# Operand chunks copied from PSUM by ScalarE, and six pairs by seven products in place of four

## The chip, the cores and the metric

The kernel runs on one core of a Trainium2 chip. The metric is device time in microseconds of one execution, as the median of a few runs. A core has five engines with instruction queues of their own: TensorE (PE in the profile; its weight loads are shown apart as PEld), VectorE (DVE), ScalarE (ACT), GpSimd (POOL) and SyncE (SP), which here issues nearly all transfers from memory. Data is computed on in SBUF; TensorE writes its results to PSUM, which has eight banks of 128 x 512 f32. This kernel keeps four banks for the sums of a product (`ps_acc`) and four for everything else (`ps_tmp`).

## The reference

One layer of an encoder block, on 256 rows (`T`) of 4096 columns (`D`), all in f32. What matters here is the chain of large products:

```
xn   = rms_norm(x)
proj = xn @ w_in                       # 4096 -> 14336: q, k, v, z_a, a_c, g_c, z_c
y_a  = rms_norm(attention(q, k, v)) * silu(z_a)          # 2048 columns
y_c  = rms_norm(conv_module(a_c, g_c)) * silu(z_c)       # 2048 columns
h    = x + concat(y_a, y_c) @ w_out                      # 4096 x 4096
gate = sigmoid(rms_norm(h) @ w_ple_gate + b_ple_gate)    # 4096 x 4096
out  = rms_norm(h + gate * (p @ w_ple))
```

The change touches the making of the left operands of two of them: `concat(y_a, y_c)` for w_out (the projection) and `h` for w_ple_gate (the last gate), and the order of work in the first product of each.

## The kernel before

**A product.** `mixed_product` computes two column blocks of 512 for both halves of the rows (four quarters, h = row half, j = column block) over the 4096 rows of a weight, which it takes in 16 pairs of 128-row blocks. Every f32 operand is split into a high part in the rounded format f32r and a low part (the rest, again f32r), and a product of two blocks is three matmuls: high x high, low x high, high x low (`add`, L380 to L391, the matmul at L385). The high part of a weight is made by ScalarE and the low part by VectorE (`parts_of`, L204 and L205); three tiles of each exist (`part_tiles`).

**Plain pairs and sevens.** A plain pair does 2 blocks x 4 quarters x 3 matmuls = 24 (`add_plain`). A pair marked `*` is done as a 2 x 2 block product with seven multiplications in place of eight (Strassen's scheme in Winograd's form): 7 x 3 = 21 matmuls. For this VectorE makes sums of the weights (`ua`, `ub`, L467, L468, L474, L475) and splits them, and the left operand's combinations of the pair's four blocks must stand ready in a second operand tile (`comb`, read by `s_of`). Three of the seven products (P2, P3, P4) go to the product's own banks, as three of a plain pair's four quarters do; the other four (P1, P5, P6, P7, the helpers) take all four `ps_tmp` banks from the first seven of a product until `on_helpers` has summed them after its last seven (`helper_sums`, L512 to L516, and sums of the caller).

**The orders.** A string such as `dense` gives the order of the 16 pairs and marks the sevens. `late` (L340) is used for the first of the four products of w_out and for the first of the four of the last gate: there the left operand is still being made while the product runs, and it is made in `ps_tmp` banks, so the sevens come late.

**Making an operand.** The left operand must stand with its columns on the partitions. `operand` (L305) makes one chunk of 512 columns of it: for each of two pairs of 128-column blocks, four transposes on TensorE into one `ps_tmp` bank (`transposed`, L170), then for each block the high part by ScalarE with the block's gain as scale (L156) and the low part by VectorE from PSUM and the high part (L157). For the first pair of a chunk the seven-product combinations are made as well: ScalarE copies one block, scaled, to a row tile (L284), VectorE makes four 128-wide combinations (L268 to L271; L269 and L271 read the other block from PSUM), and their parts are made by L276 and L277. The row tiles (tag `row`) are three in all; the loads of biases and gains (`broadcast_row`) and of the embedding input (`pin`, L1113) use them too.

`y_ahead` and `h_ahead` call `operand` for a chunk some pairs before the product reads it: chunks 0 and 1 in the last pair of the product before, chunks 2 to 7 one at a time ahead of pairs 3 to 13. After chunk 7, `h_ahead` also makes the operand of the embedding `p` (`embedding`), which still uses L156 and L157. A dependency (L494) puts all these transposes before the first helper matmul of the product.

**The order of instructions.** What is not pinned is ordered by a planner when the program is built: by the order in the code, and by when it estimates that an instruction's inputs and buffers are there. Each engine then runs its own list in that fixed order, waiting on semaphores. `later` and `fill` hand out small steps (sums of squares, multiplications by gates) between pairs.

Of the kernel before, what the change touches and what calls it, by code (L numbers as in the profile page):

```python
# [10 lines left out]
F32 = mybir.dt.float32  # L11
F32R = mybir.dt.float32r
AF = mybir.ActivationFunctionType
ALU = mybir.AluOpType
AX = mybir.AxisListType

P = 128
NB = 512
# [7 lines left out]
def hybrid_block(  # L26
# [23 lines left out]
    nc = tc.nc  # L50
    _, T, D = x.shape
# [16 lines left out]
    def pool(name, bufs, stack=ctx, side=0, **kw):  # L68
        return stack.enter_context(tc.tile_pool(name=name, bufs=bufs, side=sides[side], **kw))
# [12 lines left out]
    spool = pool("spool", 2, first_scratch, 1)  # L82
# [3 lines left out]
    def tmp_psum():  # L86
        return ps_tmp.tile([P, 512], F32, tag="tmp", name="tmp_ps")
# [61 lines left out]
    def big_tile(pool=None):  # L149
        return (pool or big).tile([P, 4, 2, T], F32R, tag="big", name="big_t")  # L150

    def split_from_psum(dst, i, src, scale):

        hi, lo = dst[:, i, 0, :], dst[:, i, 1, :]
        return (
            nc.scalar.activation(hi, src, AF.Identity, scale=scale),  # L156
            nc.vector.scalar_tensor_tensor(  # L157
                lo, src, scale, hi.bitcast(F32), ALU.mult, ALU.subtract
            ),
        )  # L160
# [3 lines left out]
    def transposed(src, blocks, then=lambda ins: None):  # L164

        pt = tmp_psum()
        for i, b in enumerate(blocks):
            for h in range(NH):
                last_transpose[:] = [
                    nc.tensor.transpose(  # L170
                        pt[:, i * T + h * P : i * T + (h + 1) * P],
                        src[:, h, b] if len(src.shape) == 4 else src[:, h, b * P : (b + 1) * P],
                        ident,
                    )
                ]
                then(*last_transpose)
        return [pt[:, i * T : (i + 1) * T] for i in range(len(blocks))]
# [80 lines left out]
    def sum_rows():  # L258
        return [spool.tile([P, NB], F32, tag="row", name="comb", bufs=3) for _ in range(2)]

    def combined_parts(dst, at, s, a, a01, a11, g, then=lambda ins: None):

        a00, a10 = a[:, :P], a[:, P:]
        s3, s5, s2, s4 = (s[:, i * P : (i + 1) * P] for i in range(4))
        stt = nc.vector.scalar_tensor_tensor
        then(nc.vector.tensor_tensor(s3, a00, a10, ALU.subtract))  # L268
        then(stt(s5, a11, g, a10, ALU.mult, ALU.subtract))  # L269
        then(stt(s2, s5, -1.0, a00, ALU.mult, ALU.subtract))  # L270
        then(stt(s4, a01, g, s2, ALU.mult, ALU.add))  # L271

        def split():
            hi, lo = dst[:, at : at + 2, 0, :], dst[:, at : at + 2, 1, :]
            src = s.rearrange("q (i t) -> q i t", t=T)
            then(nc.scalar.copy(hi, src))  # L276
            then(nc.vector.tensor_tensor(lo, src, hi.bitcast(F32), ALU.subtract))  # L277

        return split

    def combine(dst, at, pts, g):

        a, s = sum_rows()
        nc.scalar.activation(a[:, :T], pts[0], AF.Identity, scale=g[:, :1])  # L284
        combined_parts(dst, at, s, a[:, :T], pts[1][:, :P], pts[1][:, P:], g[:, 1:2])()

    def combine_again(dst, at, t, i, rows, then=lambda ins: None):

        a, s = rows
        then(  # L290
            nc.vector.tensor_tensor(
                a.rearrange("q (i t) -> q i t", t=T), t[:, i : i + 2, 0, :].bitcast(F32),
                t[:, i : i + 2, 1, :].bitcast(F32), ALU.add,
            )
        )
        return combined_parts(dst, at, s, a[:, :T], a[:, T : T + P], a[:, T + P :], 1.0, then)

    def comb_tile(combs, n_kept=0):

        if len(combs) < D // NB // 2 - 1 + n_kept:  # L300
            combs.append(big_tile(more))
        else:
            combs.append(keep.tile([P, 4, 2, T], F32R, tag="comb", name="comb_t"))

    def operand(src, g, c, tiles, combs, pool=None, combined=True):  # L305

        t = big_tile(pool)
        if c % 2 == 0:
            comb_tile(combs)
        for pair in range(2):  # L310
            blocks = (2 * pair, 2 * pair + 1)
            pts = transposed(src, blocks)
            for b, pt in zip(blocks, pts):
                split_from_psum(t, b, pt, g[:, b : b + 1])
            if pair == 0 and combined:
                combine(combs[c // 2], 2 * (c % 2), pts, g[:, :2])
        tiles.append(t)

    def pair_parts(src):
# [4 lines left out]
    def units(text):  # L324

        return [(int(u.rstrip("*+")), u[-1] if u[-1] in "*+" else "") for u in text.split()]
# [10 lines left out]
    norm = units("1 3 5 7 9 11 0+ 13 2* 15 4+ 8 6* 10 12 14")  # L337
    norm_fills = (7, 8, 8, 8, 6, 4, 2, 3, 2, 3, 2, 2, 0, 6, 5, 5)
    final = units("1 0* 3 2* 5 4* 6* 7 8* 9 10* 12* 11 13 14 15")
    late = units("1 3 5 7 9 11 13 15 0* 2 4* 6 8* 10* 12 14")  # L340

    def mixed_product(
        w, col, lhs, comb, order, on_helpers, ahead=None, fills=(0,), on_begin=None, apart=NB,
# [162 lines left out]
    tt, stt = nc.vector.tensor_tensor, nc.vector.scalar_tensor_tensor  # L506
# [53 lines left out]
    for c in range(0, 4, 2):  # L560
        if c:
            t = upool.tile([P, 4, 2, T], F32R, tag="big", name="big_t", bufs=1)
        else:
            t = keep.tile([P, 4, 2, T], F32R, tag="comb", name="comb_t")
# [3 lines left out]
    def combinations(c, then=lambda ins: None):  # L568

        rest = []  # L570

        def begin():
            rows = spool.tile([P, 2, NB], F32, tag="stage", name="comb")
            rest.append(
                combine_again(*xS[2 * c], xT[c], 0, (rows[:, 0], rows[:, 1]), then)
            )

        return begin, lambda: rest.pop()()

    def first_pairs(add):  # L580
# [62 lines left out]
        for n in range(1, n_x + 1):  # L643
# [26 lines left out]
    rows = [(conv_ln_g, KCW), (conv_ln_b, KCW), (b_dw, KCW), (attn_out_g, AW // P),  # L670
            (conv_out_g, KCW), (ple_norm_g, KD)]
    n_rows = sum(n for _, n in rows)
    at = [sum(n for _, n in rows[:i]) for i in range(len(rows))]
# [324 lines left out]
    def broadcast_row(src, n0, n, **kw):  # L998

        kw = kw or dict(tag="row", bufs=3)  # L1000
        t = spool.tile([P, n], F32, name="row", **kw)
        nc.sync.dma_start(
            t, bass.AP(tensor=src.tensor, offset=src.offset + n0, ap=[[0, P], [1, n]])
        )
        return t
# [10 lines left out]
    spool = upool = pool("lpool", 2, side=1)  # L1016
    y_c = []
    ssq_c = cpool.tile([P, NH, CW // NB], F32, name="ssq_c")
    for c0, order in zip(range(0, CW // NB, 2), point):
        row = broadcast_row(b_pw, c0 * NB, 2 * NB, tag="stage")  # L1020
        rows = [row[:, j * NB : (j + 1) * NB] for j in range(2)]
# [29 lines left out]
    for c in range(2, D // NB):  # L1051
        if c % 2 == 0:
            comb_tile(xS, 1)
        combine_again(xS[c // 2], 2 * (c % 2), xT[c], 0, sum_rows())()
# [71 lines left out]
    for c0 in range(0, D // NB, 2):  # L1126
        for j in range(2):
            hc = act.tile([P, NH, NB], F32, tag="act", name="hc")
            c = c0 + j
# [85 lines left out]
    rows, fgs = [], []  # L1215
# [51 lines left out]
    def sum_of(h, at):  # L1267
        s = end[:, 0, h : h + 1]
        pin(nc.vector.tensor_reduce(s, ssq_f[:, h, :at], AX.X, ALU.add))
        return s  # L1270
# [45 lines left out]
    s = sum_of(1, n_f + 1)  # L1316
# [35 lines left out]
```

## Time and profile before

| | |
|---|---|
| median of 3 runs | 2029.64 us (2028.74 to 2030.21) |
| profiled execution | 2028.23 us |
| its span, first to last instruction | 2026.5 us |
| granted TensorE clock, mean | 0.998 |
| first w_out product, from about | 1315 to 1405 us of the span |
| first product of the last gate, from about | 1652 to 1742 us |

In the rows of a timeline the columns are: start in the span, time from there to the end of the group's last instruction, engine, line, operation, output <- inputs, shapes, and how many instructions are merged; in brackets the idle time before it and what ended it. The times of neighbouring instructions overlap a little, because one starts while the end of the one before is still written; so the cost of an instruction in a full queue is the distance from its start to the next one's start. In the rows of one line or tile the three numbers are the shortest, median and longest duration in ns.

### The profile page before, as it was taken

What the parts mean: (1) busy time and instruction counts of PE and PEld (TensorE: products, weight loads), DVE (VectorE), ACT (ScalarE), POOL (GpSimd) and SP (SyncE); (2) the same over time, 40 slices, a digit from 0 to 9 for tenths busy, and PEclk for the clock granted to TensorE, in tenths of its full rate; (3) what the DMA queues carried; (4) which work ended last, traced back from release to release, by engine and by line L of the source; (5) the groups of instructions that cost most, each with busy time, mean ns of one, the idle gap of its engine ahead of it and who ended that gap; (6) DMA issues with size and microseconds to landing.
All of it is one profiled execution on the core that took longest, in us unless ns stands there. A gap on an engine that the chain in (4) does not pass through costs nothing.

```text
span 2026.5 us, 26195 instructions
## 1 busy us (share of the span) xinstructions
PE 2010.8 (99%) x9073; PEld 1654.4 (82%) x9073; DVE 1903.4 (94%) x2708; ACT 1215.0 (60%) x1583; POOL 46.9 (2%) x50
## 2 busy tenths in 40 slices
PE   9999999999999999999999999999999999999997
PEld 7888888888888888788888888888888888888876
DVE  7999999889999997888899999999999999999998
ACT  7655545655655555776556556666665666655555
POOL 0000000000000000000000000000000000000000
PEclk9999999999999999999999999999999999999999
DMA  8787878678678867456666666676666656666765
GB/s 295 222 238 234 255 217 250 177 247 240 188 221 246 252 198 241 156 177 209 196 208 207 208 204 211 208 239 210 203 211 197 208 194 201 208 218 207 231 207 180
DMA packets 171168, 436.70 MB, mean 215 GB/s; under 512 B 13966, under 2 KB 17182, under 8 KB 171034
## 3 DMA queue, kind: packets, MB, share of 16 engines
q1 hardware_dynamic: 161952, 417.93, 63.9%
q0 software_dynamic: 8432, 16.25, 4.8%
q8 instruction: 71, 1.16, 0.2%
q10 hardware_dynamic: 650, 0.84, 0.1%
q14 instruction: 63, 0.52, 0.1%
HBM read 430.77 MB, written 4.19 MB: 215 GB/s over the span
## 4 chain that ended last, share of the span: by engine, by line
PE 95%; DVE 3%; issue 1%; ACT 1%; DMA 0%; POOLq 0%; POOL 0%; ACTq 0%; SPq 0%; DVEq 0%
PE acc L385 73%; PE acc_P L385 17%; PE tmp_ps L170 1%; DVE cv L724 1%; PE acc L229 1%; DVE wl L205 1%; PE tmp_ps L893 0%; PE tmp_ps L877 0%; PE tmp_ps L911 0%; PE tmp_ps L916 0%; PE acc L373 0%; ACT wh L204 0%; PE tmp_ps L892 0%; DVE ul L205 0%; DMA xin<-in_x_dram 0%
## 5 line engine op out<-in xcount | busy, mean ns | idle before, releaser
L385 PE MATMUL acc<-wh,big_t 128*128 128x512 f32 x4154 | 1283.3, 391 | 0.6 <-DVE y_c L1043 0.4
L204 ACT CAST wh<-wt 128x1024 fp32r<-128x1024 f32 (+1 forms) x737 | 710.1, 974 | 523.3 <-PE acc L385 364.3
L385 PEld LDWEIGHTS acc<-wh,big_t 128*128 128x128 f32 x4154 | 777.0, 188 | 160.8 <-DVE y_c L1043 0.9
L205 DVE TENSOR_TENSOR wl<-wt,wh 128x1024 fp32r<-128x1024 f32 (+1 forms) x737 | 817.4, 1122 | 39.9 <-ACT wh L204 33.6
L385 PE MATMUL acc<-wl,big_t 128*128 128x512 f32 x2077 | 801.9, 391 | 0.1
L385 PEld LDWEIGHTS acc<-wl,big_t 128*128 128x128 f32 x2077 | 389.5, 188 | 82.5 <-DVE wl L205 1.8
L204 ACT CAST uh<-ua 128x1024 fp32r<-128x1024 f32 x174 | 182.9, 1052 | 91.1 <-DVE ua L468 46.3
L205 DVE TENSOR_TENSOR ul<-ua,uh 128x1024 fp32r<-128x1024 f32 x174 | 212.0, 1219 | 9.6 <-ACT uh L204 8.1
L724 DVE SCALAR_TENSOR_TENSOR cv<-uT,dw,cv 128x250 f32<-128x250 f32 (+19 forms) x480 | 203.6, 464 | 1.1
L385 PE MATMUL acc_P<-uh,big_t 128*128 128x512 f32 x528 | 161.8, 392 | 0.0
L204 ACT CAST uh<-ub 128x1024 fp32r<-128x1024 f32 x92 | 96.8, 1052 | 95.5 <-DVE ub L475 79.2
L205 DVE TENSOR_TENSOR ul<-ub,uh 128x1024 fp32r<-128x1024 f32 x92 | 112.2, 1220 | 6.7 <-ACT uh L204 5.6
L385 PEld LDWEIGHTS acc_P<-uh,big_t 128*128 128x128 f32 x528 | 98.0, 188 | 23.2 <-ACT uh L204 3.7
L385 PE MATMUL acc_P<-ul,big_t 128*128 128x512 f32 x264 | 101.3, 392 | 0.0
L467 DVE TENSOR_TENSOR ua<-wt 128x512 f32<-128x512 f32 x102 | 69.9, 685 | 17.3 <-DMA wt<-in_w_in_dram 10.7
L385 PE MATMUL acc<-uh,big_t 128*128 128x512 f32 x266 | 82.5, 390 | 0.0
L385 PE MATMUL acc_P<-wh,big_t 128*128 128x512 f32 x266 | 82.1, 389 | 0.0
L468 DVE TENSOR_TENSOR ua<-wt 128x512 f32<-128x512 f32 x102 | 69.6, 683 | 4.3 <-DMA wt<-in_w_in_dram 3.6
L385 PE MATMUL acc_P<-uh,comb_t 128*128 128x512 f32 x228 | 70.1, 390 | 0.1
L475 DVE TENSOR_TENSOR ub<-ub,wt 128x512 f32<-128x512 f32 x92 | 63.0, 685 | 0.8
L474 DVE TENSOR_TENSOR ub<-ua,wt 128x512 f32<-128x512 f32 x92 | 62.9, 683 | 0.3
L385 PEld LDWEIGHTS acc_P<-ul,big_t 128*128 128x128 f32 x264 | 49.3, 188 | 12.5 <-DVE ul L205 2.0
(243 smaller groups left out, 1485.5 us busy)
## 6 DMA issues: line engine op xcount, KB each, us to landing
wt<-in_w_in_dram SPq DMA_DIRECT2D x416, 512.0 KB, 4.5
wt<-in_w_out_dram SPq DMA_DIRECT2D x128, 512.0 KB, 4.3
wt<-in_w_ple_gate_dram SPq DMA_DIRECT2D x128, 512.0 KB, 4.2
wt<-in_w_pw_dram SPq DMA_DIRECT2D x32, 512.0 KB, 4.8
ua<-in_w_in_dram SPq DMA_DIRECT2D x31, 512.0 KB, 4.3
ua<-in_w_in_dram POOLq DMA_DIRECT2D x31, 512.0 KB, 8.7
wt<-in_w_in_dram SPq DMA_DIRECT2D x31, 256.0 KB, 2.8
hc<-in_x_dram SPq DMA_DIRECT2D x8, 512.0 KB, 4.7
```

What stands on the lines that cost most here:

```text
L170: nc.tensor.transpose(pt[:, i * T + h * P : i * T + (h + 1) * P], src[:, h, b] if len(src.shape) == 4 else src[:, h, b * P : (b + 1) * P], ...
L204: nc.scalar.copy(wh[:, :kc, :], wt[:, :kc, :]),
L205: nc.vector.tensor_tensor(wl[:, :kc, :], wt[:, :kc, :], wh[:, :kc, :].bitcast(F32), ALU.subtract),
L229: nc.tensor.matmul(acc, a, b[:, k, :], start=kb == 0 and kind == 0, stop=kb == kblocks - 1 and kind == 2,)
L385: nc.tensor.matmul(banks[name], a, b, start=name not in begun, stop=final and ends[name] == n and kind == 2 and not (left and name in "P2 ...
L467: plus(ua[:, 0], w0[:, 0], w0[:, 1])
L468: plus(ua[:, 1], w0[:, 1], w1[:, 1])
L474: plus(ub[:, 0], ua[:, 0], w1[:, 1])
L475: plus(ub[:, 1], ub[:, 0], w1[:, 0])
L724: nc.vector.scalar_tensor_tensor(cv[:, i, PAD - k :], uT[:, i, : T + k - PAD], dw[:, b, k : k + 1], cv[:, i, PAD - k :], ALU.mult, ALU.add,)
```

## The change

`operand` no longer makes the parts of each block from PSUM. For each pair of blocks ScalarE copies both blocks from PSUM, scaled, into one 512-wide row tile; the high parts of both are then one 512-wide cast by ScalarE from that tile, and the low parts one 512-wide subtraction by VectorE. The combinations are made from the same row tile, so their extra copy goes and all their inputs lie in SBUF. Row tiles per chunk: three (two for the pairs, one for the combinations) where there were two. `combined_parts` takes four blocks in place of one row and a gain. The order `late` has six sevens in place of four: pairs 2 and 12 become sevens beside 0, 4, 8 and 10. Pair 15 moves behind the first seven, three sevens (8, 10, 12) now stand in a row, and one plain pair (14) is left behind the last seven where there were two (12, 14).

```diff
-    def combined_parts(dst, at, s, a, a01, a11, g, then=lambda ins: None):
-        a00, a10 = a[:, :P], a[:, P:]
+    def combined_parts(dst, at, s, a00, a10, a01, a11, then=lambda ins: None):
         s3, s5, s2, s4 = (s[:, i * P : (i + 1) * P] for i in range(4))
         then(nc.vector.tensor_tensor(s3, a00, a10, ALU.subtract))
-        then(stt(s5, a11, g, a10, ALU.mult, ALU.subtract))
+        then(nc.vector.tensor_tensor(s5, a11, a10, ALU.subtract))
         then(stt(s2, s5, -1.0, a00, ALU.mult, ALU.subtract))
-        then(stt(s4, a01, g, s2, ALU.mult, ALU.add))
+        then(nc.vector.tensor_tensor(s4, a01, s2, ALU.add))
...
-    def combine(dst, at, pts, g):
-        a, s = sum_rows()
-        nc.scalar.activation(a[:, :T], pts[0], AF.Identity, scale=g[:, :1])
-        combined_parts(dst, at, s, a[:, :T], pts[1][:, :P], pts[1][:, P:], g[:, 1:2])()
+    def combine(dst, at, a):
+        s = spool.tile([P, NB], F32, tag="row", name="comb", bufs=3)
+        (a00, a10), (a01, a11) = ((a[:, i, :P], a[:, i, P:]) for i in range(2))
+        combined_parts(dst, at, s, a00, a10, a01, a11)()
...
+        rows = sum_rows()
         for pair in range(2):
             blocks = (2 * pair, 2 * pair + 1)
-            pts = transposed(src, blocks)
-            for b, pt in zip(blocks, pts):
-                split_from_psum(t, b, pt, g[:, b : b + 1])
+            a = rows[pair].rearrange("q (i t) -> q i t", t=T)
+            for i, pt in enumerate(transposed(src, blocks)):
+                b = blocks[i]
+                nc.scalar.activation(a[:, i], pt, AF.Identity, scale=g[:, b : b + 1])
+            hi, lo = (t[:, 2 * pair : 2 * pair + 2, q, :] for q in range(2))
+            nc.scalar.copy(hi, a)
+            nc.vector.tensor_tensor(lo, a, hi.bitcast(F32), ALU.subtract)
             if pair == 0 and combined:
-                combine(combs[c // 2], 2 * (c % 2), pts, g[:, :2])
+                combine(combs[c // 2], 2 * (c % 2), a)
...
-    late = units("1 3 5 7 9 11 13 15 0* 2 4* 6 8* 10* 12 14")
+    late = units("1 3 5 7 9 11 13 0* 15 2* 4* 6 8* 10* 12* 14")
```

`combine_again`, which makes combinations from parts that exist already, is only adapted to the new arguments.

More of the change, by code (lines that the diff above doesn't have):

```diff
@@ L295, in combine_again @@
         )
[L296 removed]
+        return combined_parts(dst, at, s, *(a[:, i * P : (i + 1) * P] for i in range(4)), then)
     def comb_tile(combs, n_kept=0):
```

## The prediction, made before the run

> **What bounds the kernel now.** I read the page's busy shares and its chain first, then the busy time of each engine in the two stages that use the order `late`, then those stages instruction by instruction. The page's first lines, and its chain by engine:
>
> ```profile
> span 2026.5 us, 26195 instructions
> PE 2010.8 (99%) x9073; PEld 1654.4 (82%) x9073; DVE 1903.4 (94%) x2708; ACT 1215.0 (60%) x1583; POOL 46.9 (2%) x50
> PE 95%; DVE 3%; issue 1%; ACT 1%; DMA 0%; POOLq 0%; POOL 0%; ACTq 0%; SPq 0%; DVEq 0%
> ```
>
> TensorE sets the time: it is busy for 99% of the span, so what can be gained is what is taken off its own list. VectorE at 94% is close behind. How close in the two stages the windows show (columns: window, length, then busy time of PE, PEld, DVE, ACT, POOL, clock, DMA share, GB/s). The first two rows are the first w_out product before and from the preparation of its first seven-product pair on; the last two are the same for the first product of the last gate.
>
> ```profile
> 1314.80:1357.20 42.40, 42.40 (x212) 35.33 (x211) 39.49 (x76) 31.03 (x53) 0.00 (x0) 1.00 0.73 240
> 1357.20:1399.50 42.30, 42.30 (x187) 34.86 (x187) 42.27 (x55) 24.17 (x27) 0.00 (x0) 1.00 0.65 212
> 1651.80:1701.20 49.40, 49.40 (x245) 41.31 (x244) 45.97 (x87) 35.33 (x63) 0.69 (x1) 1.00 0.57 178
> 1701.20:1735.00 33.80, 33.80 (x150) 27.99 (x150) 33.09 (x40) 20.02 (x22) 0.00 (x0) 1.00 0.71 232
> ```
>
> TensorE never pauses. VectorE has 2.9 and 3.4 us free in the halves where the operands are made, but only 0.03 and 0.7 us where the sevens run. The halves differ, and the change takes from the first and gives to the second.
>
> **The seventh-product pairs, on TensorE.** A pair by seven products has 21 matmuls, a plain pair 24. The starts of the first seven of the last gate, of the plain pair behind it, and of the next seven:
>
> ```profile
> 1701.26 0.62 PE L385 MATMUL acc_P<-wh,big_t 128*128 128x512 f32 x2
> 1706.02 0.62 PE L385 MATMUL acc<-wh,big_t 128*128 128x512 f32 x2
> 1711.45 0.62 PE L385 MATMUL acc_P<-wh,big_t 128*128 128x512 f32 x2
> ```
>
> 4.76 us against 5.43, 0.67 us less for a pair that is turned. `late` turns two (2 and 12), in two products: **-2.7 us**, twelve matmuls. Nothing else leaves TensorE; the transposes stay.
>
> **The seventh-product pairs, on VectorE.** Start to start in the w_out stage:
>
> ```profile
> 1386.56 0.68 DVE L205 TENSOR_TENSOR wl<-wt,wh 128x512 fp32r<-128x512 f32 x1
> 1387.16 0.68 DVE L475 TENSOR_TENSOR ub<-ub,wt 128x512 f32<-128x512 f32 x1
> 1387.77 1.22 DVE L205 TENSOR_TENSOR wl<-wt,wh 128x1024 fp32r<-128x1024 f32 x1
> 1388.90 1.22 DVE L205 TENSOR_TENSOR ul<-ua,uh 128x1024 fp32r<-128x1024 f32 x1
> ```
>
> A 512-wide instruction takes 0.60 us and a 1024-wide one 1.13. A plain pair needs two of 1024: 2.26 us. A seven needs five of 512 (four sums and one low part) and three of 1024: 6.39. Each pair turned costs VectorE 4.13 us, two of them 8.26 in each product, in the half where it has next to nothing free, while TensorE comes 1.34 us earlier: VectorE falls back by 9.6 us.
>
> **The operands.** Per chunk VectorE loses four low parts from PSUM of 256 and gets two from SBUF of 512; two of the four 128-wide steps of the combination read SBUF in place of PSUM.
>
> ```profile
> 1335.27 0.69 DVE L277 TENSOR_TENSOR big_t<-comb,big_t 128x512 fp32r<-128x512 f32 x1
> 1335.88 0.87 DVE L157 SCALAR_TENSOR_TENSOR big_t<-tmp_ps,prm,big_t 128x256 fp32r<-128x256 f32 x2
> 1336.67 1.21 DVE L205 TENSOR_TENSOR wl<-wt,wh 128x1024 fp32r<-128x1024 f32 x1
> L269 DVE SCALAR_TENSOR_TENSOR comb<-comb x15: 280/283/314, 28.4 to 1368.4; 128x128 f32<-128x128 f32 x15
> L269 DVE SCALAR_TENSOR_TENSOR comb<-tmp_ps,prm,comb x15: 339/344/346, 1312.4 to 1695.3; 128x128 f32<-128x128 f32 x15
> ```
>
> From the starts: two old low parts 0.79 us, one new 0.61. Four against two save 0.36, the combination 2 x 0.06: **0.48 us a chunk**, 2.9 us for the six chunks made inside each product (chunks 0 and 1 are made in the product before). But this is saved in the half where VectorE already stands idle for 2.9 us, and it cannot store the time, since only three tiles of each weight part exist:
>
> ```profile
> ACT wh L204 <- PE acc L385: 9.8, 8, 3.1
> ```
>
> (from the waits of ScalarE between 1310 and 1400 us: it waits eight times for TensorE to give a weight tile back). Only what is saved just before the first seven can be used, about one chunk of the six: I take 0.5 us, ends 0 and 2.9.
>
> ScalarE: the copies from PSUM stay four; the fifth (for the combination) goes, and two 512-wide casts from SBUF come.
>
> ```profile
> L156 ACT ACTIVATE big_t<-tmp_ps,prm x64: 459/469/483, 1308.6 to 1692.5; 128x256 fp32r<-128x256 f32 x64
> L284 ACT ACTIVATE comb<-tmp_ps,prm x15: 462/468/498, 1311.6 to 1693.8; 128x256 f32<-128x256 f32 x15
> L276 ACT CAST big_t<-comb x20: 607/617/622, 47.0 to 1683.9; 128x512 fp32r<-128x512 f32 x20
> ```
>
> -0.47 + 2 x 0.62 = +0.77 us a chunk, 4.6 us in a half where ScalarE has 11 to 14 us free: I cost it at nothing. If that cover is gone it comes out as lateness of the low parts, which is the third rival.
>
> **What this does at the end of w_out's first product.** Behind the last seven there were two plain pairs, in which VectorE makes the eight sums of the helpers; now there is one, after three sevens in a row. The end of the product before:
>
> ```profile
> 1400.63 0.68 DVE L467 TENSOR_TENSOR ua<-wt 128x512 f32<-128x512 f32 x1
> 1401.24 1.22 DVE L205 TENSOR_TENSOR wl<-wt,wh 128x1024 fp32r<-128x1024 f32 x1
> 1402.37 0.68 DVE L468 TENSOR_TENSOR ua<-wt 128x512 f32<-128x512 f32 x1
> 1402.97 0.68 DVE L474 TENSOR_TENSOR ub<-ua,wt 128x512 f32<-128x512 f32 x1
> 1403.58 2.47 DVE L1151 TENSOR_TENSOR hc<-acc,hc 128x512 f32<-128x512 f32 x4
> 1404.97 0.61 PE L385 MATMUL acc<-wh,big_t 128*128 128x512 f32 x2
> ```
>
> The next product's first matmul (1404.97) needs the bank that L1151 empties. Ahead of L1151 VectorE did three sums of 0.60 (L467, L468, L474) that are for the next seven only: 1.8 us of slack. Moving pair 15 behind the first seven helps: it is 5.43 us of TensorE for 2.26 of VectorE, 3.2 us to the good, which before fell into the half with idle time. Then 9.6 - 1.8 - 3.2 - 0.5 = 4.1 us are missing; the last of the four L1151 ends at about 1406.0 and its bank is next written 9 matmuls (2.0 us) after 1404.97, so 1.0 us may be won by emptying in another order, of which I count half: **+3.6 us** of TensorE waiting, in the last seven, the last pair and at the banks. Ends: 0, if the planner moves the combinations of chunk 7 (four steps of 0.2 and two of 0.6) and the helpers' sums behind what is urgent and puts off the matmuls with low weight parts, as it did at 1321.6; 7.3, if nothing of pair 15's surplus can be kept.
>
> ```profile
> 1321.61 1.99 PE L385 MATMUL acc<-wh,big_t 128*128 128x512 f32 x8
> 1323.68 1.17 PE L385 MATMUL acc<-wl,big_t 128*128 128x512 f32 x4
> ```
>
> **The same in the last gate.** Here 0.7 us was free in the half itself, and behind it VectorE waited for a weight and did one sum for the next seven:
>
> ```profile
> 1740.33 0.69 DVE L467 TENSOR_TENSOR ua<-wt 128x512 f32<-128x512 f32 x1 [1.43 <-DMA wt<-in_w_ple_gate_dram]
> ```
>
> Slack 0.7 + 1.43 + 0.6 = 2.7. The embedding's product, 24 matmuls on `ps_tmp` banks, stands between the last pair and the next product: 5.43 us more for VectorE, against two low parts (2.26) that the row above already holds, so what is missing, 9.6 - 2.7 - 3.2 - 0.5 = 3.2, falls into this gap but for the banks that the helpers must give back first; I take a sixth of it, **+0.5 us**, ends 0 and 3.2.
>
> This stage also makes the embedding's operand, whose transposes the code puts before the first helper matmul. Pair 15, which lay between, now comes after.
>
> ```profile
> 1693.08 0.38 SPq L1113 DMA_DIRECT2D pin<-in_p_dram  x1
> DMA to landing us min/median/max: 3.9/3.9/3.9
> 1696.67 0.28 DVE L270 SCALAR_TENSOR_TENSOR comb<-comb 128x128 f32<-128x128 f32 x1
> 1697.84 0.60 PE L170 MATMUL tmp_ps<-ident,pin 128*128 128x128 f32 x4
> 1698.19 0.48 PE L385 MATMUL acc<-wl,big_t 128*128 128x512 f32 x1
> ```
>
> Pair 13 ends at 1701.26 - 5.43 - 0.35 (the transposes) = 1695.48. The load of `pin` waits on SyncE for one of three "row" tiles. An operand now takes all three where it took two, so `pin` must wait for the last chunk's own: not 1693.08 but about when that chunk's first row was last read before, 1696.67 + 0.28 = 1696.95. Landing 1700.85, transposes to 1701.3: TensorE would be 5.8 us short of work for the helpers. It has other work: the nine matmuls of pair 0 that go to no helper and the first half of pair 15, 21 x 0.227 = 4.8 us. **+1.0 us** stays. Ends 0 and 5.8. The weight loads queued behind `pin` on SyncE are those of the pairs from 15 on, two tiles ahead: hidden, or else part of the same 5.8.
>
> **Sum.** -2.7 + 3.6 + 0.5 + 1.0 = +2.4 us on the profiled execution's 2028.23: 2030.6. The median is 1.41 above that execution, so **2032.0 us**; 0.2% (4.06 us, about what a measurement of this kernel can tell from no change) is not reached.
>
> **Rivals.**
> *All waits are hidden.* For it: TensorE stands still nowhere in the windows although VectorE is full, and its order adapts. Against it: the last low parts and the helpers' sums must still end before banks are emptied. Time: 2029.64 - 2.7 = 2026.9. A gain over 0.2% would need 1.4 us more, which TensorE does not have to give.
> *The late `pin` row makes it slower.* The 5.8 us are not covered, because pair 15's weight tiles are not there while pair 0 holds its own. -2.7 + 3.6 + 0.5 + 5.8 = +7.2: 2036.8. It decides from 2.7 us of uncovered wait on (4.06 + 2.7 - 4.1). Against it: the matmuls of pair 0 to banks of their own.
> The Trainium skill, "TensorE: Matmul & The Clock Gate", Part 1 on the clock gate, says that after about 3.4 us without work the array falls to half its clock until it was busy as long again; by an estimate from that page such a pause would cost some 1.7 us more. No row here shows a pause of that length between matmuls: the clock in all four windows is 1.00.
> *The low parts come late.* A low part now follows two copies and a 512-wide cast: 0.62 + 0.69 - 0.48 = 0.83 us later than a 256-wide one from PSUM. Chunk 6 of w_out, its transposes, its last low part, and the pair that reads it:
>
> ```profile
> 1345.90 1.04 PE L170 MATMUL tmp_ps<-ident,y_c 128*128 128x128 f32 x8
> 1352.25 0.47 DVE L157 SCALAR_TENSOR_TENSOR big_t<-tmp_ps,prm,big_t 128x256 fp32r<-128x256 f32 x1
> 1353.06 0.70 PE L385 MATMUL acc<-wh,big_t 128*128 128x512 f32 x2
> ```
>
> Spare time 1353.06 - 1352.72 = 0.34. Over by 0.5 us for twelve chunks is 6 us, beside the 4.1 of the two product ends: -2.7 + 6 + 4.1 = +7.4, 2037.0. It decides from 0.34 us of lateness on. Against it: the late block is the pair's second, read 2.7 us on.
> The Trainium skill, "Perfetto Trace Analysis", section Optimizing Scalar/DVE Operations, has both sides of this: larger operations raise the throughput of a saturated engine, but where such an engine only causes pauses on another, smaller pieces can finish sooner. VectorE at 93% in the first halves is nearer to the first case; by the second this rival would hold.
>
> **How the numbers follow.** Forecast 0.44 (its own range 2029.5 to 2035.5; 0.33 of it within 0.2%, 0.11 above), all hidden 0.28 (0.03 of it faster by over 0.2%), late row 0.18 (0.16 slower), late low parts 0.10 (0.09 slower). Faster 0.03, same 0.33 + 0.25 + 0.02 + 0.01 = 0.61, slower 0.11 + 0.16 + 0.09 = 0.36. Range: from the matmuls alone, 2026.9, less 0.4 us (the runs before lie between 2028.74 and 2030.21), 2026.5, to both w_out's and the row's upper ends, -2.7 + 7.3 + 5.8 = +10.4, 2040.0; the ends leave out about 1 in 10.
>
> **What would show it.** Twelve matmuls fewer; 0.6 us of VectorE for a new low part; TensorE waiting for VectorE (low parts, L1151) between the third seven in a row and the second product of w_out, about 3.6 us; less, 0.5, in the last gate; the `pin` load later behind its chunk, with a pause of 1 us before the first helper matmul. Pauses in the first halves would speak for late low parts; no pause anywhere, and the ledger of VectorE is wrong.

## The result and the profile after

| | before | the change |
|---|---|---|
| median of runs side by side | 2030.21 us (2028.74 to 2032.04) | 2037.31 us (2036.83 to 2038.44) |
| ratio to before | | 1.0037 (95% interval 1.0026 to 1.0049) |
| profiled execution, its span | 2028.23, 2026.5 us | 2037.99, 2036.2 us |

The change makes the kernel 0.37% slower, some 7.5 us by the ratio (the two medians are 7.1 apart): inside the range of the prediction (2026.5 to 2040.0), but 5 us above its value, and on the other side of the 0.2% within which it was forecast. The page of the changed kernel, its busy times and its chain:

```profile
span 2036.2 us, 26216 instructions
PE 2014.6 (99%) x9061; PEld 1650.5 (81%) x9061; DVE 1912.7 (94%) x2700; ACT 1231.9 (60%) x1608; POOL 47.0 (2%) x50
PE 88%; DVE 6%; issue 2%; DMA 2%; ACT 1%; SPq 0%; POOLq 0%; POOL 0%; ACTq 0%; DVEq 0%
```

TensorE has its twelve matmuls less (9073 to 9061) and still shows 99%. Its time outside of busy (span less busy) grew from 15.7 to 21.6 us, and its busy time by 3.8 although matmuls went, so part of the loss hides in what is counted as busy. The number of matmuls in a window shows it better. The chain shows more: before, 95% of it ran over TensorE, 3% over VectorE; now 88% and 6%.

The windows of the changed kernel (the same columns as before): the first half of w_out's first product, then its sevens and the beginning of the second product.

```profile
1340.00:1360.00 20.00, 20.00 (x101) 16.69 (x100) 18.26 (x30) 16.53 (x28) 0.00 (x0) 1.00 0.70 231
1360.00:1380.00 20.00, 19.29 (x84) 15.25 (x83) 19.16 (x27) 11.98 (x14) 0.00 (x0) 1.00 0.65 209
1380.00:1400.00 20.00, 18.80 (x82) 15.01 (x82) 19.91 (x26) 12.03 (x14) 0.00 (x0) 1.00 0.58 192
1400.00:1420.00 20.00, 19.25 (x84) 15.38 (x83) 19.73 (x26) 12.00 (x19) 0.00 (x0) 1.00 0.59 180
```

The half in which the operands are made has no pause, and VectorE has 1.7 us free in it. The pauses begin with the sevens. They go on past 1407.9 us, where the second product begins, which the change does not touch. The same in the last gate: 30 us of its second product, which uses the order `dense`, in the changed kernel,

```profile
1760.00:1770.00 10.00, 9.09 (x37) 6.30 (x36) 9.34 (x12) 5.59 (x11) 0.00 (x0) 1.00 0.48 154
1770.00:1780.00 10.00, 9.51 (x42) 7.31 (x41) 10.00 (x14) 5.51 (x8) 0.00 (x0) 1.00 0.68 211
1780.00:1790.00 10.00, 8.55 (x37) 6.32 (x36) 9.32 (x13) 7.42 (x9) 0.00 (x0) 1.00 0.72 236
```

and in the kernel before:

```profile
1760.00:1770.00 10.00, 10.00 (x44) 7.91 (x44) 10.00 (x14) 6.83 (x10) 0.00 (x0) 1.00 0.58 188
1770.00:1780.00 10.00, 10.00 (x45) 8.25 (x45) 10.00 (x13) 7.29 (x8) 0.00 (x0) 1.00 0.67 235
1780.00:1790.00 10.00, 9.96 (x44) 7.74 (x44) 9.96 (x13) 5.11 (x7) 0.00 (x0) 1.00 0.73 224
```

116 matmuls where there were 133. What TensorE waited for in the changed kernel (microseconds in total, times, longest), in w_out's first two products (the first two rows) and in the last gate's (the other three); for the kernel before the same view has no row in either stretch.

```profile
PE acc_P L389 <- DVE ul L205: 1.9, 3, 0.7
PE acc L389 <- DVE hc L1155: 0.8, 1, 0.8
...
PE acc_P L389 <- ACT uh L204: 2.2, 3, 1.4
PE acc L389 <- DVE wl L205: 0.5, 1, 0.5
PE tmp_ps L170 <- DMA pin<-in_p_dram: 0.4, 1, 0.4
```

(L389, L1155 and L1117 are the lines L385, L1151 and L1113 of before.)

**Where the time went, stage by stage.** For each matmul of a run I take its start less the start of the matmul at the same place in the program of before (counted back from the end, with the matmuls that the run has fewer allowed for). The table has how much this lag grows over each stage, so a stage with six matmuls fewer and no wait would show -1.4 (6 x 0.227). It is used for the runs below, but for the two with sums by transfer. Each row rests on one execution. The runs enter these stages between 0.3 us ahead of the kernel before and 2.7 us behind it; that difference is left out.

| run | w_out, product 1 | product 2 | products 3, 4 | gate, product 1 | product 2 | rest |
|---|---|---|---|---|---|---|
| the change | +1.8 | +1.8 | +0.1 | -0.1 | +4.4 | +0.4 |
| operands alone | +0.6 | 0.0 | 0.0 | +1.3 | +1.2 | -0.2 |
| order alone | +1.9 | +5.1 | +0.4 | +1.2 | +4.9 | +0.4 |
| six in w_out only | +2.1 | +1.7 | -0.2 | +1.2 | +0.4 | +0.5 |
| six in the gate only | +0.8 | 0.0 | -0.2 | +0.1 | +4.8 | +0.5 |
| four, own home for `pin` | +0.4 | 0.0 | -0.1 | +0.3 | +0.8 | -0.1 |
| six, own home for `pin` | +1.9 | +1.9 | -0.2 | -0.3 | +3.2 | +0.4 |
| five, own home for `pin` | +2.4 | +0.1 | -0.2 | -0.4 | +0.8 | 0.0 |
| six, pair 15 last, own home | +2.5 | +0.5 | -0.1 | +1.8 | +1.6 | +0.3 |
| the change, four sums less | +2.4 | +1.7 | -0.2 | +1.7 | +0.9 | -0.2 |
| before, four sums less | -0.1 | +0.1 | +0.5 | 0.0 | -0.9 | -0.5 |

More than half of the loss, 6.2 us (1.8 + 4.4), falls into the two products behind those that were changed. Not all of it is the sevens': with the operands alone, the gate's second product has +1.2 already.

The longest pauses of w_out, in the changed kernel:

```profile
1377.07 0.50 PE L389 MATMUL acc_P<-ul,big_t 128*128 128x512 f32 x1 [0.71 <-DVE ul L205]
1380.54 0.50 PE L389 MATMUL acc_P<-ul,big_t 128*128 128x512 f32 x1 [0.45 <-DVE ul L205]
1398.92 0.50 PE L389 MATMUL acc_P<-ul,comb_t 128*128 128x512 f32 x1 [0.74 <-DVE ul L205]
1410.41 0.73 PE L389 MATMUL acc<-wh,big_t 128*128 128x512 f32 x2 [0.75 <-DVE hc L1155]
```

The first two stand in the seven of pair 4, which follows that of pair 2 at once. The third stands in the last seven (pair 12), and the fourth at a bank of the second product, 2.5 us after its start.

**How the debt is handed on.** The longest pause in the last gate, in the changed kernel: TensorE's row,

```profile
1788.42 0.73 PE L389 MATMUL acc_P<-uh,big_t 128*128 128x512 f32 x2 [1.35 <-ACT uh L204]
```

and ScalarE's list ahead of it:

```profile
1785.12 1.06 ACT L204 CAST wh<-wt 128x1024 fp32r<-128x1024 f32 x1 [1.37 <-DMA wt<-in_w_ple_gate_dram]
1786.38 1.05 ACT L204 CAST wh<-wt 128x1024 fp32r<-128x1024 f32 x1 [0.20 <-DMA wt<-in_w_ple_gate_dram]
1787.33 1.04 ACT L204 CAST uh<-ub 128x1024 fp32r<-128x1024 f32 x1
```

The sum that this cast of `ub` reads had ended at about 1785.6 (VectorE's L479 starts at 1784.92 and is 0.68 long). But the cast stands behind two casts of weights on ScalarE, and those wait for loads. The loads are late because a weight tile comes free when VectorE has made its low part. What SyncE's queue waited for around this stage (1745 to 1790 us), before,

```profile
SPq L440 <- DVE wl L205: 13.7, 9, 3.4
```

and in the changed kernel:

```profile
SPq L444 <- DVE wl L205: 18.9, 8, 5.3
```

The queue's waits for tiles of sums fell at the same time, from 21.5 to 19.7 us, so all its waits together grew by less, from 38.2 to 41.5.

By this reading, VectorE's lateness comes to TensorE by way of a weight tile, a load, and ScalarE's list: the row names ScalarE, which had only been waiting itself. No run changed the weight tiles, so that this chain sets the whole 4.4 us is read from the trace and not shown by an experiment.

### The profile page after: what moved, and what is told of

The parts are those of the page before. It is cut to its first block, busy times and chain, and to the rows that moved or that the text cites. A ratio compares the mean times of both kernels' runs of the same rounds, so it can differ in the third digit from the quotient of the medians.

```text
span 2036.2 us, 26216 instructions
## 1 busy us (share of the span) xinstructions
PE 2014.6 (99%) x9061; PEld 1650.5 (81%) x9061; DVE 1912.7 (94%) x2700; ACT 1231.9 (60%) x1608; POOL 47.0 (2%) x50
## 3 DMA queue, kind: packets, MB, share of 16 engines
q8 instruction: 71, 1.16, 0.2%
## 4 chain that ended last, share of the span: by engine, by line
PE 88%; DVE 6%; issue 2%; DMA 2%; ACT 1%; SPq 0%; POOLq 0%; POOL 0%; ACTq 0%; DVEq 0%
PE acc L389 68%; PE acc_P L389 17%; DVE wl L205 2%; DVE cv L728 1%; DMA wt<-in_w_in_dram 1%; PE tmp_ps L170 1%; DVE ul L205 1%; PE acc L229 1%; ACT wh L204 0%; PE tmp_ps L897 0%; PE tmp_ps L881 0%; PE tmp_ps L915 0%; PE tmp_ps L920 0%; DMA wt<-in_w_ple_gate_dram 0%; DMA wt<-in_w_ple_dram 0%
## 5 line engine op out<-in xcount | busy, mean ns | idle before, releaser
L389 PE MATMUL acc<-wh,big_t 128*128 128x512 f32 x4102 | 1269.4, 391 | 1.2 <-DVE hc L1155 0.8
L389 PEld LDWEIGHTS acc<-wh,big_t 128*128 128x128 f32 x4102 | 767.0, 188 | 161.3 <-DVE hc L1155 1.8
L389 PE MATMUL acc<-wl,big_t 128*128 128x512 f32 x2051 | 792.1, 391 | 0.8 <-DVE wl L205 0.5
L389 PEld LDWEIGHTS acc<-wl,big_t 128*128 128x128 f32 x2051 | 384.4, 188 | 83.9 <-DVE wl L205 4.6
L204 ACT CAST uh<-ua 128x1024 fp32r<-128x1024 f32 x178 | 187.0, 1051 | 92.3 <-DVE ua L472 47.4
L205 DVE TENSOR_TENSOR ul<-ua,uh 128x1024 fp32r<-128x1024 f32 x178 | 216.7, 1218 | 10.8 <-ACT uh L204 9.2
L389 PE MATMUL acc_P<-uh,big_t 128*128 128x512 f32 x540 | 166.1, 394 | 2.3 <-ACT uh L204 2.2
L204 ACT CAST uh<-ub 128x1024 fp32r<-128x1024 f32 x96 | 100.9, 1051 | 96.1 <-DVE ub L479 80.4
L389 PEld LDWEIGHTS acc_P<-uh,big_t 128*128 128x128 f32 x540 | 99.4, 188 | 28.4 <-ACT uh L204 8.9
L205 DVE TENSOR_TENSOR ul<-ub,uh 128x1024 fp32r<-128x1024 f32 x96 | 117.1, 1220 | 5.5 <-ACT uh L204 4.8
L389 PE MATMUL acc_P<-ul,big_t 128*128 128x512 f32 x270 | 103.4, 393 | 1.2 <-DVE ul L205 1.2
L471 DVE TENSOR_TENSOR ua<-wt 128x512 f32<-128x512 f32 x106 | 72.6, 685 | 17.6 <-DMA wt<-in_w_in_dram 14.8
L389 PE MATMUL acc<-uh,big_t 128*128 128x512 f32 x274 | 85.0, 390 | 0.0
L389 PE MATMUL acc_P<-wh,big_t 128*128 128x512 f32 x274 | 84.6, 389 | 0.0
L472 DVE TENSOR_TENSOR ua<-wt 128x512 f32<-128x512 f32 x106 | 72.4, 683 | 3.0 <-DMA wt<-in_w_in_dram 1.4
L389 PE MATMUL acc_P<-uh,comb_t 128*128 128x512 f32 x240 | 73.9, 391 | 0.0
L479 DVE TENSOR_TENSOR ub<-ub,wt 128x512 f32<-128x512 f32 x96 | 65.8, 685 | 0.8
L389 PEld LDWEIGHTS acc_P<-ul,big_t 128*128 128x128 f32 x270 | 50.6, 188 | 14.9 <-DVE ul L205 4.3
```

What stands on the lines that cost most here:

```text
L204: nc.scalar.copy(wh[:, :kc, :], wt[:, :kc, :]),
L205: nc.vector.tensor_tensor(wl[:, :kc, :], wt[:, :kc, :], wh[:, :kc, :].bitcast(F32), ALU.subtract),
L389: nc.tensor.matmul(banks[name], a, b, start=name not in begun, stop=final and ends[name] == n and kind == 2 and not (left and name in "P2 ...
L471: plus(ua[:, 0], w0[:, 0], w0[:, 1])
L472: plus(ua[:, 1], w0[:, 1], w1[:, 1])
L479: plus(ub[:, 1], ub[:, 0], w1[:, 0])
```

## The experiments

Two theories at first. The debt: two more sevens put VectorE so far behind that its lateness is paid at the ends of the two products and behind them. The rivals: the operand code itself, or the late `pin`.

**The parts alone.** The new operand code with the old order; and the old operand code with the new order:

```diff
 (the change)
-    late = units("1 3 5 7 9 11 13 0* 15 2* 4* 6 8* 10* 12* 14")
+    late = units("1 3 5 7 9 11 13 15 0* 2 4* 6 8* 10* 12 14")

 (the kernel before)
-    late = units("1 3 5 7 9 11 13 15 0* 2 4* 6 8* 10* 12 14")
+    late = units("1 3 5 7 9 11 13 0* 15 2* 4* 6 8* 10* 12* 14")
```

> The new operand code with the old order late (four sevens). Theory 1, VectorE's debt: the sevens cost the time and the operand code nothing, so 2029.5 to 2031.5 us, within 0.1% of the kernel before, and no wait of TensorE over 0.5 us in the first products of w_out and of the last gate. Theory 2, late low parts or row tiles: the operand code costs the time, 2034 to 2038 us, with waits of TensorE in the first halves of those products.

> The old operand code with the new order late (six sevens). Theory 1: as slow as the change or slower, since VectorE keeps some 0.5 to 3 us of work per product that the operand code would save: 2036 to 2042 us, the loss in the same places. Theory 2: 2027 to 2030 us, the twelve matmuls are gained.

Measured: 2031.82 us, ratio 1.0011 (1.0002 to 1.002), and 2041.18 us, 1.0054 (1.004 to 1.0067). The first is just above the range of its first theory (2031.5) and far below that of the second. So the order makes the loss, and the operand code gives part of it back: 0.0017 of 2029.5, 3.5 us less with it than without. The size is uncertain, since the two intervals (1.004 to 1.0067, and 1.0026 to 1.0049 for the change) overlap, though the slowest run of the change (2038.44) is below the fastest of the order alone (2040.63). The saving fits VectorE's (six chunks in each product, 0.48 us each by the prediction's rows, 5.8 us in all), which it can use where it is behind. Where VectorE is not behind, with four sevens, the new code gains nothing and costs about 2 us (0.4 to 4 by the interval), most of it in the last gate.

**Six sevens in one of the two products.** The change, with a second order string, the old one, for the gate and for w_out in turn:

```diff
+    late_four = units("1 3 5 7 9 11 13 15 0* 2 4* 6 8* 10* 12 14")
...
-        gated_pair(c0, dense if c0 else late, None if c0 else h_ahead)
+        gated_pair(c0, dense if c0 else late_four, None if c0 else h_ahead)
```

> The change, but the first product of the last gate has the old order with four sevens; w_out has six. Theory 1: about half of the loss stays, +3 to +4 us on the kernel before (2033 to 2034.5), paid in the first two products of w_out, and the products of the last gate step by less than 1 us. Theory 2: +5 us or more, since the operand code is in both.

> The change, but the first product of w_out has the old order with four sevens; the last gate has six. Theory 1: +4 to +5 us on the kernel before (2034 to 2035.5), most of it not in the first product of the last gate but in the second, which starts without VectorE's lead. Theory 2: +5 us or more, with loss in w_out too.

Measured: 2034.69 us and 2034.66 us, both 1.0022 (1.0013 to 1.0031). Each product's order costs 2.9 us over the operands alone, and the costs add: 2034.69 + 2034.66 - 2031.82 = 2037.5, the change. In the table each has its loss, beyond that of the operands alone, in its own two products, and the gate's is all in the second.

**The home of `pin`.** The embedding's input goes into the tile that the helpers' sums use later, not into a row tile; with four sevens and with six:

```diff
-        pin = spool.tile([P, NH, PLE], F32, tag="row", name="pin", bufs=3)
+        pin = sums_home[0][:, :, :PLE]
...
-        _, z = sum_tiles()
+        homes, z = sum_tiles()
+        sums_home[:] = homes
```

> The new operand code, the old order (four sevens), and the embedding input loaded into a tile that is free (the one that later holds the helpers' sums) in place of a row tile. Row theory: what the operand code alone cost (2.3 us) came from the load that waits on SyncE for a row tile with the weight loads queued behind it; then it is gone, 2029 to 2030 us, TensorE's 0.4 us wait for pin is gone, and VectorE's waits for w_ple_gate weights between 1700 and 1760 us fall from 5.7 us to under 2.5. Rival, the operand code's latency or its casts cost it: 2031.5 to 2032.5 us as before.

> The change with the embedding input in that other tile, six sevens. Debt theory: the sevens' 8.3 us of VectorE per product remain the cause; only the 0.6 us pause before the helpers goes, and 0 to 2 us with it: 2035 to 2037 us. If the row were what slows the last gate in the change, 2032 to 2034 us.

Measured: 2031.06 us, 1.0007 (0.9998 to 1.0016), and 2036.17 us, 1.0031 (1.002 to 1.0043): 0.8 us less with four and 1.2 (0.0006 of 2030) with six. Neither difference is clear of the intervals, but with six most of the loss plainly stays. With four the time fell between the ranges of both theories, and VectorE's waits for weights between 1700 and 1760 us, expected to fall from 5.7 us to under 2.5, fell only to 4.6, so the load of `pin` is not what mainly delays the weights. The load does wait for a row tile: SyncE's wait ahead of `pin` before,

```profile
SPq L1113 <- DVE big_t L157: 0.6, 1, 0.6
```

and in the changed kernel:

```profile
SPq L1117 <- DVE comb L270: 2.8, 1, 2.8
```

The pause is small because the load is not as late as forecast. The rows, with the landing time of `pin`:

```profile
1694.90 0.71 PE L389 MATMUL acc<-wh,big_t 128*128 128x512 f32 x2
1699.47 0.38 SPq L1117 DMA_DIRECT2D pin<-in_p_dram  x1
DMA to landing us min/median/max: 2.6/2.6/2.6
1700.44 0.62 PE L389 MATMUL acc<-wh,big_t 128*128 128x512 f32 x2
1700.89 0.44 PE L389 MATMUL acc<-wl,big_t 128*128 128x512 f32 x1
1701.17 0.63 PE L389 MATMUL acc<-wh,big_t 128*128 128x512 f32 x2
1702.24 0.63 PE L170 MATMUL tmp_ps<-ident,pin 128*128 128x128 f32 x4 [0.44 <-DMA pin<-in_p_dram]
```

The 24 matmuls of pair 13 run from 1694.90 to 1700.44. The load is issued 1.0 us ahead of their end, where the forecast had it 1.5 us behind, and lands in 2.6 us where the kernel before had 3.9. So the transposes start 1.8 us behind pair 13, and five other matmuls (1.1 us) stand between. Two matmuls of 0.23 from 1701.17 would have let the transposes start at 1701.63: 0.6 us of pause. Of what stays with four sevens, 1.3 us over the table's row, 0.8 is in the gate's second product, and no run separates its cause.

**Less work for VectorE.** Four additions of 512 (four times 0.60 = 2.4 us) left out behind the gate's first product, in the change and, as a control, in the kernel before:

```diff
-            todo.append(partial(tt, hc, hc, gt, ALU.add))
+            if c0:
+                todo.append(partial(tt, hc, hc, gt, ALU.add))
```

> The change, with four additions of 0.60 us left out on VectorE: those that add the gated embedding to h for the first pair of column blocks of the last gate, which run during its second product (so the output is not the reference's there). Debt theory: VectorE sets the pace in that product, so the 2.4 us come off one for one: 1.8 to 2.6 us below the change, 2034.7 to 2035.5. Rival, the planner's order or the casts' latency sets it: less than 0.8 us.

> The kernel before with the same four additions left out (the same part of the output is not the reference's). Debt theory: there VectorE has a lead and TensorE does not wait, so nothing is gained: within 0.6 us of the kernel before. If VectorE's work cost time one for one everywhere, 2.4 us less.

Measured: 2035.44 us, 1.003 (1.0018 to 1.0041), and for the control 2027.51 us, 0.9992 (0.9983 to 1.0). Both are 1.9 us less than without the edit, and the control was expected to gain less than 0.6. By the medians the pair therefore tells nothing apart: VectorE's time in this stage is worth something in the kernel before as well, though no wait of TensorE shows there. The table leans to the debt, with 1.7 us less over the gate's two products in the change (4.3 to 2.6, with the second product at 0.9 in place of 4.4) against 0.9 in the control, but that is near the difference of two executions.

**The amount or the order.** Three more runs have the own home for `pin`. Five sevens, the sixth taken back:

```diff
-    late = units("1 3 5 7 9 11 13 0* 15 2* 4* 6 8* 10* 12* 14")
+    late = units("1 3 5 7 9 11 13 0* 15 2* 4* 6 8* 10* 12 14")
```

> The change with the embedding's input in the tile of the sums, and five sevens in `late` (0, 2, 4, 8, 10; pairs 12 and 14 plain behind the last). Against four sevens, with the same home for the embedding's input (2031.06), each of the two products has 0.67 us of TensorE less and 4.13 + 0.67 = 4.8 us of VectorE more to catch up. Theory 1, the ledger with a threshold: 1.8 to 2.7 us of slack and 3.2 from pair 15 are used up first, so nothing is waited for: 2029 to 2031. Theory 2, every us that VectorE falls back costs from the first on: half of what six cost, 2033 to 2034.

Measured: 2030.84 us, 1.0006 (0.9997 to 1.0015), against 2031.06 with four and 2036.17 with six. By the medians the fifth costs nothing, the sixth 5 us: not a price per us of debt, but slack that is used up first. In the table nothing is handed on to the second products (+0.1 and, as with four, +0.8), and in the gate's first product the fifth seven brings what its three matmuls are worth (+0.3 to -0.4). In w_out it loses 2 us inside the product, with these waits between 1310 and 1410 us:

```profile
PE acc_P L389 <- DVE ul L205: 1.2, 2, 0.7
```

They stand in the seven of pair 4, right behind that of pair 2, where the changed kernel has them too. So "costs nothing" is a loss in w_out and a gain in the gate, and a threshold alone does not describe w_out. The edit also takes away the third of the three sevens in a row (8, 10, 12). No run has six sevens without three in a row, so what that row costs beside the amount stays open.

Six sevens with pair 15 at the end, two plain pairs behind the last seven as there were before:

```diff
-    late = units("1 3 5 7 9 11 13 0* 15 2* 4* 6 8* 10* 12* 14")
+    late = units("1 3 5 7 9 11 13 0* 2* 4* 6 8* 10* 12* 14 15")
```

> The change with the embedding's input in the tile of the sums, and pair 15 at the end: 0* 2* 4* 6 8* 10* 12* 14 15, so two plain pairs stand behind the last of the six sevens as they did behind the last of the four. The same work for every engine. Theory 1, the sum of VectorE's work between the first seven and the end of the product counts, wherever pair 15 stands in it: 2035.5 to 2037. Theory 2, the short end is what costs: 2032 to 2034.5. Rival: six sevens with a single plain pair between them run VectorE's tiles dry, and the stall moves into the middle: 2037.5 to 2040.

Measured: 2036.24 us, 1.0033 (1.002 to 1.0046), the same as with pair 15 behind the first seven. By the table, where the plain pair stands mainly decides in which product the debt is paid: it has +2.5 and +0.5 in w_out where it had +1.9 and +1.9, +1.8 and +1.6 in the gate where it had -0.3 and +3.2. So it is not the short end that costs; the amount fits.

Sums of weights made by an accumulating transfer from GpSimd's queue in place of VectorE, for three of the six sevens, and as a control for two of the four of the kernel before:

```diff
-    late = units("1 3 5 7 9 11 13 0* 15 2* 4* 6 8* 10* 12* 14")
+    late = units("1 3 5 7 9 11 13 0* 15 2* 4+ 6 8+ 10* 12+ 14")

 (the kernel before)
-    late = units("1 3 5 7 9 11 13 15 0* 2 4* 6 8* 10* 12 14")
+    late = units("1 3 5 7 9 11 13 15 0* 2 4+ 6 8+ 10* 12 14")
```

> The change with the embedding's input in the tile of the sums, and three of the six sevens (4, 8, 12) with their two first sums of the weights made by the transfer (an accumulating DMA from GpSimd's queue, as the products before attention have it) in place of VectorE: 3 x 2 x 0.60 = 3.6 us less for VectorE in each product, everything else the same. Theory 1, VectorE's debt sets the loss: the 9.6 us fall to 6.0 and some 1.5 to 2.5 us come back in each product, 2031.5 to 2033.5. Theory 2, it is not the amount of VectorE's work but the order at the end (three sevens in a row, one plain pair behind): as without it, 2035.5 to 2037. Should the added transfers be late, slower than that.

> Control: the kernel before with two of its four sevens in `late` (4 and 8) made by the accumulating transfer in the same way: 2 x 2 x 0.60 = 2.4 us of VectorE less in each of the two products. Theory 1, VectorE owed nothing there: 2028.5 to 2030.5. Theory 2, VectorE's work in these two products counts even before, as the control with four sums less suggested (1.9 us for 2.4 us of VectorE): 2025.5 to 2028.

Measured: 2048.92 us, 1.0097 (1.0084 to 1.0111), and 2036.02 us, 1.0033 (1.0021 to 1.0045): both much slower than either theory, so neither says what VectorE's time is worth. Nor is everything else the same in them. The code that takes a `+` in an order gives up the second tile of sums of a seven (`ub`), also for the sevens marked `*`, and makes the second sums in place in `ua`. Between 1355 and 1405 us, in the kernel before and in the control:

```profile
L475 DVE TENSOR_TENSOR ub<-ub,wt x4: 681/684/684, 1362.4 to 1387.2; 128x512 f32<-128x512 f32 x4
L475 DVE TENSOR_TENSOR ua<-ua,wt x4: 687/690/693, 1364.3 to 1395.5; 128x512 f32<-128x512 f32 x4
```

The second sums must then wait until the first were read. How much of the loss is this and how much the transfers, no run separates. The transfer needs a tile of sums early, and there are two. In the control ScalarE waits for it (1350 to 1420 us),

```profile
ACT uh L204 <- DMA ua<-in_w_out_dram: 6.2, 1, 6.2
```

and in the run with six, ahead of the last gate's fourth seven, GpSimd can issue the transfer only when VectorE has given a tile back:

```profile
1720.94 1.21 POOL L425 DMA_DIRECT2D ua<-in_w_ple_gate_dram  x1 [19.14 <-DVE wl L205]
```

With the landing that the tile's transfers have there,

```profile
DMA to landing us min/median/max: 5.4/8.2/9.4
```

it arrives at about 1729. The cast that reads it starts then (its row names TensorE, whose last matmul ended at the same time), and the cast of the next weight stands behind it. ScalarE's rows:

```profile
1729.63 1.04 ACT L204 CAST uh<-ua 128x1024 fp32r<-128x1024 f32 x1 [7.58 <-PE acc L389]
1730.58 0.61 ACT L204 CAST wh<-wt 128x512 fp32r<-128x512 f32 x1
```

None of the runs that do the whole work is faster than the kernel before; the control that leaves additions out is lower, with an interval that reaches 1.0.

## Why the prediction was right and wrong

- **Twelve matmuls fewer, -2.7 us: held.** 9073 to 9061.
- **VectorE's ledger: held in size.** Two products with two more sevens each at 4.13, 16.5 us, less 0.48 for each of the sixteen chunks (chunks 0 and 1, made in the products before, count here too), makes about 8.8 us; the busy time grew by 9.3 (1903.4 to 1912.7). A new low part takes 0.60 from start to start, as forecast:

```profile
1332.87 0.68 DVE L318 TENSOR_TENSOR big_t<-comb,big_t 128x512 fp32r<-128x512 f32 x1
1333.47 1.21 DVE L205 TENSOR_TENSOR wl<-wt,wh 128x1024 fp32r<-128x1024 f32 x1
```

- **The operand's saving, 0.5 us of it usable in a product: too small.** Order alone against the change puts it at about 3.5 us for two products where the prediction had 1.0. The mistake made the forecast too high, by itself.
- **The rest of the operand code, costed at nothing: not shown to hold.** With four sevens and `pin` apart the code costs 1.7 us (1.0007, interval 0.9998 to 1.0016, so nothing is not excluded; 1.3 in the table's row).
- **w_out, +3.6 us: mechanism right, size short, place partly wrong.** The table gives 1.8 + 1.8, and 1.4 of matmuls less were gained there: 5.0 us, inside the stated ends (0 to 7.3). Against four sevens, both with the own home for `pin`, it is 3.8 - 0.4 + 1.4 = 4.8 by the table, where the ledger had 4.1 missing and counted 3.6. The waits at the bank (`hc`, 0.75) and in the last seven (`ul`, 0.74) are where they were forecast. The other two, 1.16 together, come earlier, in the seven of pair 4.
- **The last gate, +0.5 us: this is the step that failed.** With `pin` apart it measured about 4.5: 4.3 in its two products and 1.4 for the matmuls gained, less 1.2 of `pin`. With four sevens and the own home for `pin` 1.1 of this stands there too; against that run the two more sevens cost 2.9 - 1.1 + 1.4 = 3.2, each figure from one execution. That is all that the ledger had missing (3.2 us): the debt was sized about right, and its cover was not there. The prediction let the embedding's product, 24 matmuls for which VectorE has nothing urgent, take all but a sixth. It did cover the first product's end (-0.1). But the next product pays +4.4. As the trace reads, that time is needed at once for its sums and low parts, and it starts with its tiles late. The prediction asked where a product ends late and stopped at the product's end.
- **`pin`, +1.0 us: held in size, by luck.** 1.2 by the ratios, whose intervals overlap, and a pause of 0.6 in the trace; the wait is where it was said to be. But the gap to cover was 1.8 us and not 5.8, and five matmuls covered it, not 21: two errors that nearly cancel. The rival of 5.8 us uncovered falls with the gap.
- **Late low parts: the rival falls.** No pause in w_out's first half (20.00 of 20.00 in the window from 1340), and no wait of TensorE in the gate's ahead of the `pin` transposes.
- **All waits hidden: falls,** with the waits above.

With the measured terms: -2.7 + 5.0 + 4.5 + 1.2 = +8.0, against the forecast's +2.4 and the 7.5 of the ratio (0.0037 of 2030). These terms hold what the operand code costs by itself. The range held because w_out's and the row's upper ends were in it; the chance of "slower", 0.36, was too low because the forecast itself took the gate's cover for granted.

The Trainium skill, "Perfetto Trace Analysis", section Optimizing Scalar/DVE Operations, cited in the prediction for both sides of larger operations, agrees with the runs on the side of the saturated engine: the operand code with the 512-wide low parts helped where VectorE was behind (order alone against the change, about 3.5 us).

## What to carry to other kernels

When two engines are both near full, keep a ledger of the second one over the stage and over the one behind it: what it owes at the end of a stage is paid where the next stage wants its first inputs, and a gap in between hides it only if the next stage does not need that same time. Slack can be used up first and paid for later: by the medians the fifth seven cost nothing here and the sixth 5 us, so try one step less before giving up an idea, or before extending one. And look at the matmuls in a window, not at a busy share of 99%, for the pauses of an engine that is pipelined.

## What was not expected of the hardware

TensorE's clock fell to half after two pauses close together, none longer than 1.7 us. In the run with six sevens by transfer, 2 us windows of the last gate (the last three figures are the clock, the DMA share and GB/s):

```profile
1728.00:1730.00 2.00, 1.59 (x8) 0.97 (x6) 0.00 (x0) 0.37 (x1) 0.00 (x0) 1.00 1.01 354
1730.00:1732.00 2.00, 0.73 (x2) 0.30 (x2) 1.29 (x2) 1.20 (x2) 0.68 (x1) 1.00 0.12 45
1732.00:1734.00 2.00, 1.41 (x5) 1.18 (x6) 1.83 (x3) 0.03 (x1) 0.55 (x1) 0.86 0.31 33
1734.00:1736.00 2.00, 1.24 (x3) 0.42 (x2) 0.95 (x1) 2.00 (x3) 0.00 (x0) 0.50 0.90 120
1736.00:1738.00 2.00, 1.75 (x3) 1.00 (x4) 2.00 (x4) 1.43 (x2) 0.00 (x0) 0.50 1.08 304
1738.00:1740.00 2.00, 2.00 (x6) 1.55 (x5) 2.00 (x4) 0.69 (x1) 0.00 (x0) 0.50 0.88 262
1740.00:1742.00 2.00, 2.00 (x9) 1.62 (x9) 1.97 (x3) 1.03 (x3) 0.00 (x0) 0.93 0.71 225
```

with these waits in the same run:

```profile
1731.25 0.73 PE L389 MATMUL acc_P<-wh,big_t 128*128 128x512 f32 x2 [1.66 <-ACT wh L204]
1732.59 0.50 PE L389 MATMUL acc_P<-wl,big_t 128*128 128x512 f32 x1 [0.61 <-DVE wl L205]
```

Matmuls that follow one another then start 0.43 us apart where 0.23 is usual, for about 6 us. In w_out the same run shows it after waits of 0.93 and 0.72 us. The Trainium skill, "TensorE: Matmul & The Clock Gate", Part 1, speaks of an idle window of about 3.4 us. Here no single wait is longer than 1.66 us, though the two of the last gate lie within 3.4 us of each other; that it is the share of work in such a window that counts would fit, and no run here tested it. The changed kernel's pauses, 1.4 us at most and far apart, left its clock at 1.00.
